# PSUM accumulators as pairs of banks for plain groups and as single banks for the seven products

## The chip, the core and the metric

The kernel runs as one program on one NeuronCore of a Trainium2 chip. The metric is device time in microseconds (us) from start to end of one execution. The core has TensorE (PE, matrix products), VectorE (DVE), ScalarE (ACT), GpSimd (POOL) and SyncE (SP), each of which works through its own instructions in order; waits between them are semaphores. TensorE writes its results into PSUM, which this kernel uses as 8 banks of 128 x 512 f32; DVE and ACT read them from there.

## The reference

One layer of a decoder step over 512 prompt positions and 8 sample positions that share weights (520 columns in all, `T`). The input is normalised and multiplied by one wide weight matrix `w_in`; its columns feed an attention branch (A), a gated mixing branch (B) and two merge gates:

```
h = rmsnorm(x, norm_in_g) @ w_in            # split into q, k, v, q_idx, w_idx, k_idx, z_a, u, v_b, z_b, g_a, g_b
o_a = sparse attention over the top-k keys  ;  o_b = u * (tril(W_s) @ layernorm(v_b) + b)
y_a = (o_a * silu(z_a)) @ w_proj_a          ;  y_b = (o_b * silu(z_b)) @ w_proj_b
mix = sigmoid(g_a) * y_a + sigmoid(g_b) * y_b
y   = rmsnorm(x + mix @ w_out, norm_f_g)
```

All of it is f32. What matters here is the part with `z_a`, `g_a` and `g_b`: 520 x 2048 times 2048 x 256 products, one for each 256 columns of `w_in`.

## The kernel before

**Precision.** Each f32 product is three passes: both operands are split into a high and a low part (`whi`, `wlo` for weights, `hT_hi`, `hT_lo` for the normalised input, which lies transposed in SBUF), and high x high, low x high and high x low are added in PSUM.

**Chunks.** The work of TensorE is a list of chunks, made once by `build()`. A plain group is 256 weight columns: two halves of 128, each in one or two chunks of 8 contraction tiles. Its result, 128 x 520, needs two banks (260 columns in each), so `pair_banks()` gives it a PSUM tile `pm` of 128 x 2 x 512; the pool `psm` holds two such tiles, four banks. The other four banks are the pool `pss` of small single-bank tiles (transposes, attention, sample work), which the change leaves alone.

**Seven products.** 17 groups in the middle of the list (two of `z_a`, seven of `g_b`, eight of `g_a`) use a scheme with seven products of half-size operands instead of eight. A group is seven chunks in the order `SEVEN`; a chunk is 8 contraction tiles x 3 passes = 24 matmuls that write 128 x 260, one bank. So there are 119 such chunks in a row, 2856 matmuls, all at line 338. For them `one_bank()` hands out the two banks of one `pm` tile in turn: the first chunk of a pair takes a new tile and its bank 0, the second takes bank 1 of the same tile. The right-hand operands are `hT_hi`/`hT_lo` quadrants or prepared sums `Fh`/`Fl`. Before the 119 chunks stands a plain group of `g_b`, behind them come the plain groups of `w_proj_a` (operands `oh`/`ol`), then `w_out`.

**What follows a chunk.** `seven_after` (lines 367 to 385) takes the finished bank out of PSUM: depending on the step ACT copies it to `s` or `c` (lines 367, 369, 372), or DVE adds it to an `s` or `c` tile (all DVE work has line 86, that of a helper). Step 5 adds two more DVE operations over `c` and `s` and an activation (line 381), step 6 another (line 385).

**Order.** The loop at the end of the kernel writes the order by hand. Before chunk i's matmuls it issues the split of the weights of chunk i+3 and the evacuation of chunk i-1:

```
while seven and ahead < i + SLOOK:                          # SLOOK = 3
    ahead += 1
    split(ahead, then=follow if pending else None)          # follow() issues the evacuation of chunk i-1
follow()
ps = main_chunk(i, ...)
```

Within a split of a seven chunk the order is: ACT rounds the raw weights to `whi` (line 257), then the evacuation of chunk i-1 (`then`), then DVE computes `wlo`, then up to two DVE additions `raw<-raw` that make the operand of a later step. Splits of plain chunks (the last three before the list leaves the seven chunks) have ACT `whi` and DVE `wlo` both ahead of the evacuation. `whi` and `wlo` have four buffers each, so the split of chunk i+3 starts when TensorE is through with chunk i-1.

**Waits.** Semaphore waits are not in the source. They follow from which instruction touches which tile: a matmul that writes into a PSUM tile waits for earlier readers of that tile, and the first write into a tile of a pool waits for the release of what lay there before.

Of the kernel before, what the change touches and what calls it, by code (L numbers as in the profile page):

```python
# [6 lines left out]
F32 = mybir.dt.float32  # L7
# [7 lines left out]
P = 128  # L15
# [45 lines left out]
def kernel(  # L61
# [31 lines left out]
    wspl = ctx.enter_context(tc.tile_pool(name="wspl", bufs=4))  # L93
    pools = {}
    dram = ctx.enter_context(tc.tile_pool(name="scratch", bufs=1, space=bass.MemoryType.DRAM))
    psm = ctx.enter_context(tc.tile_pool(name="psm", bufs=2, space=bass.MemoryType.PSUM))
    pss = ctx.enter_context(tc.tile_pool(name="pss", bufs=4, space=bass.MemoryType.PSUM))
    ctx.enter_context(tc.manual_schedule())
    half = {}


    def pair_banks():
        return psm.tile([P, 2, 512], F32, name="pm")

    def one_bank():
        if "t" in half:
            return half.pop("t")[:, 1, :]
        half["t"] = pair_banks()
        return half["t"][:, 0, :]

    xp = x_prompt[0]
    xs = x_sample.rearrange("b o d -> (b o) d")
# [191 lines left out]
    def rows_chunk(ch):  # L304
        hi, lo = spl_tiles["rows", ch["kq"]]
        c = ch["c"]
        if c is None and ch["first"]:
            state["ps"] = [pair_banks() for _ in range(2)]
        elif ch["first"]:
            state["ps"] = SB("rowp")  # L310
        for k in range(4):
            if k == 2:
                for job in state.pop("mid", ()):
                    next(job)
                    start(job)
            rh, rl = ch["rhs"](ch["kq"] * 4 + k)
            for u in range(2) if c is None else (0,):
                for j, (w, a) in enumerate(((hi, rh), (hi, rl), (lo, rh))):
                    flags = dict(start=ch["first"] and k == 0 and j == 0, stop=ch["last"] and k == 3 and j == 2)
                    if c is None:  # L320
                        nc.tensor.matmul(state["ps"][u][:, 0, :COLS_N], lhsT=w[:, k, u * P:(u + 1) * P],  # L321
                                         rhs=a[:, :COLS_N], **flags)
                    else:
                        nc.tensor.matmul(state["ps"][:, :2 * P], lhsT=a[:, off(c):off(c) + P], rhs=w[:, k, :], **flags)  # L324
        return state["ps"]

    def main_chunk(i, hook=None):
        ch = chunks[i]
        if ch["rows"]:
            return rows_chunk(ch)  # L330
        if ch.get("seven"):
            ps = one_bank()
            out = ps[:, :HALF]
            hi, lo = spl_tiles.pop((ch["raw"], ch["step"]))
            for k in range(8):
                rh, rl = ch["group"]["forms"](ch["f"], k)
                for j, (w, a) in enumerate(((hi, rh), (hi, rl), (lo, rh))):
                    nc.tensor.matmul(out, lhsT=w[:, k, :], rhs=a, start=k == 0 and j == 0,  # L338
                                     stop=k == 7 and j == 2)
            return ps  # L340
        if ch["first"]:
            state["ps"] = pair_banks()
        ps = state["ps"]
        hi, lo = spl_tiles.pop((ch["raw"], ch["u"]))
        for k in range(8):
            kt = ch["kc"] * 8 + k
            if hook is not None:
                hook(kt)
            rh, rl = ch["rhs"](kt)
            passes = ((hi, rh), (hi, rl), (lo, rh))[:2 if ch["evac"] is packed else 3]  # L350
            for j, (w, a) in enumerate(passes):
                for t0, t1, bank, o in ch["cuts"]:
                    nc.tensor.matmul(ps[:, bank, o:o + t1 - t0], lhsT=w[:, k, :], rhs=a[:, t0:t1],  # L353
                                     start=(ch["first"] and k == 0 and j == 0),
                                     stop=(ch["last"] and k == 7 and j == len(passes) - 1))
        return ps
# [1396 lines left out]
    while jobs:  # L1753
        for j in list(jobs):
            if next(j, 0) == 0:
                jobs.remove(j)


_INS = ["x_prompt", "x_sample", "cache_k", "cache_v", "cache_k_idx", "page_table", "norm_in_g", "w_in",
# [24 lines left out]
```

## Time and profile before

| | us |
|---|---|
| median of three runs | 1613.24 (1610.81 to 1613.37) |
| the profiled execution | 1622.19 |
| its span in the profile | 1620.5 |
| PE busy | 1512.1 (93%) |
| DVE busy | 982.9 (61%) |
| ACT busy | 580.3 (36%) |
| POOL busy | 314.3 (19%) |
| mean granted TensorE clock | 0.987 of full speed |

Times in the rows count from the span's start. A matmul's row shows its whole passage (0.28 us at full clock), and consecutive ones overlap: TensorE's pace is read from one start to the next. The clock is granted at full speed (2.4 GHz) or half (1.2 GHz).

### The profile page before, as it was taken

How to read it: one execution, taken by the hardware profiler on the slowest of the kernel's cores; microseconds unless marked ns; L12 is line 12 of the kernel's file. 1: busy time of each engine (PE TensorE's matmuls, PEld its weight loads, DVE VectorE, ACT ScalarE, POOL GpSimd, SP SyncE). 2: the span in 40 equal slices, each digit the busy share in tenths (PEclk: the TensorE clock that was granted, in tenths of full speed). 3: DMA queues.
4: the chain of work that ended last, by engine and by line, in shares of the span. 5: the costliest groups of instructions: out<-in, count | busy, mean ns of one | idle time of the engine just before them, and what ended most of it. 6: DMA issues, size and time to landing. Idle time of an engine off the chain costs nothing. (4 is left out here: it accounts for less than half of the span.)

```text
span 1620.5 us, 28341 instructions
## 1 busy us (share of the span) xinstructions
PE 1512.1 (93%) x11814; PEld 1488.8 (92%) x11814; DVE 982.9 (61%) x1844; ACT 580.3 (36%) x929; POOL 314.3 (19%) x429
## 2 busy tenths in 40 slices
PE   5999999999999899999999888888888889999997
PEld 5999999999999899999999788887888889999997
DVE  7545458989997334557567667766666665523224
ACT  6534333333222133434433333333333342323323
POOL 3000027872000400055301001010000023201111
PEclk9999999999999999999999999999999999999999
DMA  6333334455232223247542334343232458532222
GB/s 190 127 111 105 104 114 137 131 170 134 79 130 79 94 72 112 72 140 239 164 151 96 120 99 157 100 136 111 92 125 85 137 183 280 186 122 88 70 79 106
DMA packets 156579, 203.63 MB, mean 126 GB/s; under 512 B 7684, under 2 KB 138108, under 8 KB 156444
## 3 DMA queue, kind: packets, MB, share of 16 engines
q1 hardware_dynamic: 136292, 139.74, 26.8%
q0 software_dynamic: 20160, 62.09, 11.5%
q8 instruction: 92, 1.51, 0.4%
q14 instruction: 35, 0.29, 0.1%
HBM read 176.90 MB, written 24.91 MB: 125 GB/s over the span
## 5 line engine op out<-in xcount | busy, mean ns | idle before, releaser
L86 DVE TENSOR_TENSOR wlo<-raw,whi 128x1024 fp32r<-128x1024 f32 (+2 forms) x311 | 386.3, 1243 | 134.8 <-ACT whi L141 74.5
L353 PE MATMUL pm<-hT_hi,whi 128*128 128x260 f32 (+1 forms) x1648 | 378.5, 297 | 2.0 <-issue 2.0
L353 PE MATMUL pm<-hT_lo,whi 128*128 128x260 f32 (+1 forms) x1648 | 370.2, 293 | 4.0 <-DVE hT_lo L86 2.4
L353 PE MATMUL pm<-hT_hi,wlo 128*128 128x260 f32 (+1 forms) x1632 | 365.3, 293 | 0.8 <-issue 0.8
L353 PEld LDWEIGHTS pm<-hT_lo,whi 128*128 128x128 f32 x1648 | 264.2, 189 | 5.9 <-DVE hT_lo L86 3.2
L353 PEld LDWEIGHTS pm<-hT_hi,whi 128*128 128x128 f32 x1648 | 264.4, 189 | 2.6 <-issue 1.9
L353 PEld LDWEIGHTS pm<-hT_hi,wlo 128*128 128x128 f32 x1632 | 261.0, 189 | 0.9 <-issue 0.9
L141 ACT ACTIVATE whi<-raw 128x1024 fp32r<-128x1024 f32 (+2 forms) x192 | 193.4, 1009 | 94.4 <-PE pm L353 74.8
L257 ACT ACTIVATE whi<-raw 128x1024 fp32r<-128x1024 f32 x119 | 126.0, 1059 | 260.3 <-PE pm L338 128.8
L338 PE MATMUL pm<-hT_hi,whi 128*128 128x260 f32 x544 | 162.0, 298 | 34.6 <-DVE c L86 30.3
L338 PE MATMUL pm<-hT_lo,whi 128*128 128x260 f32 x544 | 158.5, 291 | 0.0
L338 PE MATMUL pm<-hT_hi,wlo 128*128 128x260 f32 x544 | 158.2, 291 | 0.0
L338 PE MATMUL pm<-Fh,whi 128*128 128x260 f32 x408 | 118.6, 291 | 37.0 <-ACT s L367 14.0
L338 PEld LDWEIGHTS pm<-hT_hi,whi 128*128 128x128 f32 x544 | 107.6, 198 | 41.2 <-DVE c L86 28.9
L338 PEld LDWEIGHTS pm<-Fh,whi 128*128 128x128 f32 x408 | 77.5, 190 | 42.4 <-ACT s L367 15.9
L338 PE MATMUL pm<-Fl,whi 128*128 128x260 f32 x408 | 115.9, 284 | 0.0
L338 PE MATMUL pm<-Fh,wlo 128*128 128x260 f32 x408 | 115.6, 283 | 0.0
L338 PEld LDWEIGHTS pm<-hT_lo,whi 128*128 128x128 f32 x544 | 107.6, 198 | 0.0
L338 PEld LDWEIGHTS pm<-hT_hi,wlo 128*128 128x128 f32 x544 | 107.4, 198 | 0.0
L353 PE MATMUL pm<-oh,whi 128*128 128x260 f32 x512 | 103.5, 284 | 0.0
L353 PE MATMUL pm<-ol,whi 128*128 128x260 f32 x512 | 103.1, 283 | 0.0
L353 PE MATMUL pm<-oh,wlo 128*128 128x260 f32 x512 | 102.8, 282 | 0.0
(504 smaller groups left out, 2771.5 us busy)
## 6 DMA issues: line engine op xcount, KB each, us to landing
raw<-in_w_in_dram SPq DMA_DIRECT2D x91, 1024.0 KB, 5.0
raw<-in_w_out_dram SPq DMA_DIRECT2D x16, 1024.0 KB, 5.3
raw<-in_w_proj_b_dram SPq DMA_DIRECT2D x8, 1024.0 KB, 7.2
raw<-in_w_proj_a_dram SPq DMA_DIRECT2D x8, 1024.0 KB, 6.7
yd<-y POOLq DMA_DIRECT2D x16, 260.0 KB
ld<-yd POOLq DMA_DIRECT2D x16, 260.0 KB
sigd<-c POOLq DMA_DIRECT2D x16, 260.0 KB
ld<-sigd POOLq DMA_DIRECT2D x16, 260.0 KB
```

The source lines that it names most:

```text
L86: return f(out, *a, **k)
L141: nc.scalar.activation(hi, src, AF.Copy)
L257: nc.scalar.activation(hi, src, AF.Copy)
L338: nc.tensor.matmul(out, lhsT=w[:, k, :], rhs=a, start=k == 0 and j == 0, stop=k == 7 and j == 2)
L353: nc.tensor.matmul(ps[:, bank, o:o + t1 - t0], lhsT=w[:, k, :], rhs=a[:, t0:t1], start=(ch["first"] and k == 0 and j == 0), stop=(ch["last ...
```

## The change

`psm` is no longer opened once with two pairs. A function `banks(kind)` opens a pool of its own for each mode and closes the one before it when the mode changes: two pairs for plain chunks (and for the `w_out` rows), four single-bank tiles for the seven products. The same four banks are used in both. Over the list the mode changes twice: from pairs to singles before the first of the 119 chunks, and back before the first `w_proj_a` chunk.

```diff
-    psm = ctx.enter_context(tc.tile_pool(name="psm", bufs=2, space=bass.MemoryType.PSUM))
     pss = ctx.enter_context(tc.tile_pool(name="pss", bufs=4, space=bass.MemoryType.PSUM))
     ctx.enter_context(tc.manual_schedule())
-    half = {}
+    mains = {}
+
+    def banks(kind):
+        if mains.get("kind") == kind:
+            return
+        if "cm" in mains:
+            mains["cm"].__exit__(None, None, None)
+        mains["n"] = mains.get("n", 0) + 1
+        cm = tc.tile_pool(name=f"psm{mains['n']}", bufs=2 if kind == "pair" else 4, space=bass.MemoryType.PSUM)
+        mains.update(kind=kind, cm=cm, pool=cm.__enter__())
 
     def pair_banks():
-        return psm.tile([P, 2, 512], F32, name="pm")
+        banks("pair")
+        return mains["pool"].tile([P, 2, 512], F32, name="pm")
 
     def one_bank():
-        if "t" in half:
-            return half.pop("t")[:, 1, :]
-        half["t"] = pair_banks()
-        return half["t"][:, 0, :]
+        banks("one")
+        return mains["pool"].tile([P, 512], F32, name="pone")
...
+    mains["cm"].__exit__(None, None, None)
```

No instruction is added, removed or moved: on each of the five engines the two programs have the same instructions in the same order (8797 listed rows on PE in both). What differs is which tile a matmul writes, and so what it waits for. The number behind a name is that of the buffer.

TensorE where the first seven chunk ends and the second begins, before: both chunks write tile 9992.

```order
L338 MATMUL pm_9992<-hT_lo_93,whi_9844 128x260
L338 MATMUL pm_9992<-hT_hi_92,wlo_9845 128x260
L338 MATMUL pm_9992<-Fh_9197,whi_9912 128x260 [waits Activation_49]
L338 MATMUL pm_9992<-Fl_9198,whi_9912 128x260
L338 MATMUL pm_9992<-Fh_9197,wlo_9913 128x260 [waits DVE_49]
L338 MATMUL pm_9992<-Fh_9197,whi_9912 128x260
```

The same six now:

```order
L345 MATMUL pone_9996<-hT_lo_90,whi_9844 128x260
L345 MATMUL pone_9996<-hT_hi_89,wlo_9845 128x260
L345 MATMUL pone_10038<-Fh_9197,whi_9912 128x260
L345 MATMUL pone_10038<-Fl_9198,whi_9912 128x260
L345 MATMUL pone_10038<-Fh_9197,wlo_9913 128x260 [waits DVE_49]
L345 MATMUL pone_10038<-Fh_9197,whi_9912 128x260
```

The second chunk has a tile of its own, and its first matmul no longer waits for ScalarE; in the built program that wait was for the ACT copy of tile 9992 to `s`, the evacuation of the first chunk. The wait on DVE, for `wlo` of its own weights, stays.

TensorE where the fifth seven chunk ends and the sixth begins, before: again one tile, and a wait for VectorE.

```order
L338 MATMUL pm_10131<-hT_lo_93,whi_10025 128x260
L338 MATMUL pm_10131<-hT_hi_92,wlo_10026 128x260
L338 MATMUL pm_10131<-hT_hi_92,whi_10062 128x260 [waits DVE_49]
L338 MATMUL pm_10131<-hT_lo_93,whi_10062 128x260
L338 MATMUL pm_10131<-hT_hi_92,wlo_10063 128x260
L338 MATMUL pm_10131<-hT_hi_92,whi_10062 128x260
```

The same six now:

```order
L345 MATMUL pone_10137<-hT_lo_90,whi_10029 128x260
L345 MATMUL pone_10137<-hT_hi_89,wlo_10030 128x260
L345 MATMUL pone_10167<-hT_hi_89,whi_10067 128x260 [waits Activation_49]
L345 MATMUL pone_10167<-hT_lo_90,whi_10067 128x260
L345 MATMUL pone_10167<-hT_hi_89,wlo_10068 128x260 [waits DVE_49]
L345 MATMUL pone_10167<-hT_hi_89,whi_10067 128x260
```

Before, the sixth chunk's first matmul waited for the DVE addition that takes the fifth chunk out of tile 10131. Now it waits for an ACT instruction, by its count the copy that empties the bank four chunks back, and the third matmul waits for the DVE instruction that makes its own `wlo`.

At the two changes of mode the built program has these waits. The first matmul of the first seven chunk waited for the evacuation of the plain chunk result two tiles back; now it waits for the one just finished (`sg<-pm`, line 1249 before), since the whole pool of pairs must be free. The first matmul of the first `w_proj_a` chunk waited for the DVE evacuation of the last seven chunk but one; now it waits for that of the last one.

## Rows read from the trace of the kernel before

**Rows 1.** The page: busy us (share) x instructions of each engine

```profile
PE 1512.1 (93%) x11814; PEld 1488.8 (92%) x11814; DVE 982.9 (61%) x1844; ACT 580.3 (36%) x929; POOL 314.3 (19%) x429
```

**Rows 2.** Waits of PE, longest first: us in total, times, longest

```profile
PE pm L338 <- DVE c L86: 30.3, 25, 2.7
PE pm L338 <- ACT s L367: 14.0, 9, 3.1
PE pm L338 <- ACT c L372: 12.2, 9, 1.4
PE pm L338 <- ACT s L369: 10.8, 8, 1.4
...
PE pm L338 <- DVE s L86: 4.4, 8, 0.7
```

**Rows 3.** Stretches: us; busy us of PE, PEld, DVE, ACT, POOL; PEclk; DMA; GB/s

```profile
38.00:200.00 162.00, 161.96 (x947) 159.30 (x948) 80.13 (x126) 68.60 (x132) 2.09 (x3) 1.00 0.35 114
...
887.50:1328.60 441.10, 369.47 (x2857) 357.49 (x2856) 294.50 (x339) 168.05 (x217) 33.57 (x62) 0.97 0.37 121
```

**Rows 4.** Timeline of PE across two chunk boundaries: start, us, instruction [idle before]

```profile
1317.10 0.28 PE L338 MATMUL pm<-Fh,wlo 128*128 128x260 f32 x1
1317.22 0.28 PE L338 MATMUL pm<-hT_hi,whi 128*128 128x260 f32 x1
...
1319.97 0.28 PE L338 MATMUL pm<-hT_hi,wlo 128*128 128x260 f32 x1
1322.94 0.39 PE L338 MATMUL pm<-hT_hi,whi 128*128 128x260 f32 x1 [2.68 <-DVE c L86]
1323.17 0.28 PE L338 MATMUL pm<-hT_lo,whi 128*128 128x260 f32 x1
```

**Rows 5.** Timeline of DVE and of PE around one of the 2.3 us waits

```profile
959.67 2.49 DVE L86 TENSOR_TENSOR raw<-raw 128x1024 f32<-128x1024 f32 x2
962.07 0.42 DVE L86 TENSOR_TENSOR c<-pm,s 128x260 f32<-128x260 f32 x1
...
962.54 0.39 PE L338 MATMUL pm<-hT_hi,whi 128*128 128x260 f32 x1 [2.32 <-DVE c L86]
```

**Rows 6.** Stretches: around a drop of the clock, then two of 50 us

```profile
895.10:898.40 3.30, 3.30 (x18) 3.30 (x17) 3.13 (x4) 0.45 (x1) 0.00 (x0) 0.50 0.67 235
...
1100.00:1150.00 50.00, 41.95 (x338) 40.54 (x337) 34.98 (x41) 18.81 (x24) 3.19 (x6) 1.00 0.34 112
1150.00:1200.00 50.00, 41.96 (x325) 40.54 (x324) 31.51 (x35) 17.94 (x23) 1.64 (x4) 0.97 0.33 106
```

**Rows 7.** Timeline at the first seven chunk, PE and ACT

```profile
887.53 0.28 PE L338 MATMUL pm<-hT_hi,whi 128*128 128x260 f32 x1
...
888.77 0.58 ACT L1249 ACTIVATE sg<-pm 128x520 f32<-128x520 f32 x1
...
893.25 0.37 ACT L367 ACTIVATE s<-pm 128x260 f32<-128x260 f32 x1
...
893.67 0.39 PE L338 MATMUL pm<-Fh,whi 128*128 128x260 f32 x1 [3.09 <-ACT s L367]
```

**Rows 8.** Timeline at the last seven chunk, DVE and PE

```profile
1327.13 1.22 DVE L86 TENSOR_TENSOR wlo<-raw,whi 128x1024 fp32r<-128x1024 f32 x1 [3.64 <-ACT whi L141]
...
1329.87 0.43 DVE L86 TENSOR_TENSOR c<-pm,c 128x260 f32<-128x260 f32 x1
...
1328.64 0.28 PE L338 MATMUL pm<-hT_hi,wlo 128*128 128x260 f32 x1
1328.84 0.47 PE L353 MATMUL pm<-oh,whi 128*128 128x260 f32 x2
```

**Rows 9.** DVE in 887.5 to 1328.6 by groups: count, busy us, mean ns, idle before

```profile
L86 DVE TENSOR_TENSOR wlo<-raw,whi 128x1024 fp32r<-128x1024 f32 x120 | 146.7, 1223 | 59.5 <-ACT whi L257 52.5 <-ACT whi L141 7.0
L86 DVE TENSOR_TENSOR raw<-raw 128x1024 f32<-128x1024 f32 x66 | 80.9, 1225 | 2.3
```

**Rows 10.** The page's weight loads: KB each, us from issue to landing

```profile
raw<-in_w_in_dram SPq DMA_DIRECT2D x91, 1024.0 KB, 5.0
```

## The prediction

> **What bounds the kernel now.** I read the page's table of engines first: PE is busy 93% of the span, DVE 61% [rows 1], so only PE's waits are worth time, and 108 us of the span are not PE work. The list of PE's waits says where most of those 108 us lie: five kinds of wait at line 338, the seven products, 30.3 + 14.0 + 12.2 + 10.8 + 4.4 = 71.7 us in 25 + 9 + 9 + 8 + 8 = 59 waits [rows 2]. Each is for an evacuation out of PSUM (DVE into `c` or `s`, ACT into `s` or `c`), none for weights or for a transfer. The view by stretches then shows what the stage is worth: in the 441.1 us of the seven products PE runs 2857 matmuls at a mean clock of 0.97, DVE is busy 294.5 us and ACT 168.0 [rows 3]. Last, the timeline. At 1317.22 a chunk begins 0.12 us behind the matmul before it, the ordinary step; the next chunk begins at 1322.94, 2.97 us behind the one at 1319.97, and PE sat idle for 2.68 us of that [rows 4]. 59 waits over 119 chunks is every second boundary: the second chunk of each pair, which writes the other bank of the tile that is just being emptied. First chunks of a pair, which take a fresh tile, do not wait.
>
> Why the wait is long is seen on DVE: an evacuation that DVE could do in 0.42 us starts at 962.07, behind two additions of raw weights that occupied DVE for 2.49 us from 959.67, and PE goes on at 962.54 after 2.32 us of idling [rows 5]. TensorE thus pays for the place of the evacuation in another engine's order.
>
> **The change part by part.** It removes and adds no instruction; it changes waits in three places.
>
> First, inside the seven products. Chunk i has a bank of its own and waits for the evacuation of chunk i-4, which is issued ahead of chunk i-3 and has three chunks' time to finish. The 59 waits go. I size this from the stage's own pace. A chunk without a wait takes 1319.97 - 1317.22 + 0.12 = 2.87 us [rows 4]; 119 of them are 341.5 us. The stage lasts from 887.53 [rows 7] to 1328.84 [rows 8], 441.3 us. The difference is 99.8 us. The parts confirm it: 71.7 us of waits as listed; for each wait 0.16 us more, since the list counts from the end of a 0.28 us passage and the next step would have come after 0.12, 9.4 us; the second matmul behind a wait comes 0.23 us after the first instead of 0.12 [rows 4], 6.5 us; and the clock, granted at half speed in stretches such as 895.10 to 898.40, where 3.30 us hold 18 matmul rows [rows 6]: a mean of 0.97 over 441.1 us is 0.03 x 441.1 = 13 us lost. Together 100.6 us.
>
> Do the drops of the clock go too? In 1100 to 1150 us no drop falls and 338 matmuls run; in 1150 to 1200 one does, and 325 run [rows 6]. The first drop stands right behind the longest wait, 3.09 us to 893.67 [rows 7]. In 38 to 200 us, where PE is busy 161.96 of 162.00 us, the clock stays at 1.00 [rows 3]. I take it that without waits it stays there: all 13 us return. Bounds: none of it to all of it.
>
> Second, the first seven chunk. The pool of pairs must be empty before the singles open, so its first matmul, now at 887.53, waits for the sigmoid of the last plain chunk, which on ACT starts at 888.77 and takes 0.58 us. A matmul released by ACT starts 0.05 us behind its end (893.25 + 0.37 to 893.67) [rows 7]: 889.40, so 1.87 us, and 0.11 for the start after a wait. Queued behind the waiting matmul is all of PE's stage, so the price is paid in full. Bounds: 0, if the sigmoid came earlier, which its place behind a `whi` excludes; and 3.6 us, if the wait costs a drop of the clock (half of a 3.3 us stretch as in [rows 6] lost). It cannot be a gain, since PE has nothing else to do.
>
> Third, the first `w_proj_a` chunk waits for the evacuation of the last seven chunk. DVE does it at 1329.87, 0.43 us long [rows 8], the last of five operations in its queue since 1327.13; with the same 0.05 us PE would go on at 1330.35 instead of 1328.84: 1.5 us, plus 0.11. The last chunk but one no longer waits its 2.68 us [rows 4], but DVE's five operations hang on that chunk's end in either program, so the distance stays. Bounds: 0 to 3.2, as above.
>
> What is late next? On DVE, 294.5 / 17 = 17.3 us of work per group of seven chunks against 7 x 2.87 = 20.1 us [rows 3]: 86%, no longer slack by a third. Its longest burst is the split of a first step: `wlo` and two additions, 1.22 + 2.49 us [rows 5, 9], behind an evacuation of 0.42, and begun some 1.1 us after the chunk's end because `whi` comes first; that is 5.2 us against a chunk of 2.87, so DVE falls 2.4 us behind and recovers in the two light steps that follow. The `wlo` is wanted three chunks later, 8.6 us, and the bank too. ACT has 168.0 / 17 = 9.9 us per group. The weights: two loads of 1024 KB per group at 5.0 us each [rows 10] are 10 us of 20.1, and the tighter one, issued after the fourth step's split, is needed at the next group's first split, four chunks or 11.5 us later. I take nothing for any of these.
>
> Sum: -99.8 + 1.98 + 1.6 = -96.2 us on the profiled execution, 1622.19 (span 1620.5), that is 1526.0. That execution stands 9.0 us over the median of the runs, 1613.24; I carry the same difference and predict 1517 us.
>
> **The rivals.**
>
> A, DVE becomes the bound of the stage. For it: 86% of the new stage, and `wlo` already has 59.5 us of idling for `whi` in front of it [rows 9]. If all of that idling survived, the stage could not be shorter than 294.5 + 59.5 = 354 us, 12.5 more than 341.5: 1530 us. Against it: that idling is mostly DVE being early.
>
> B, the clock goes on dropping. The step from one accumulator to another is a short pause at each chunk, and if such pauses, not the waits of 1.4 to 3.1 us, cost the clock, the 13 us stay: 1530 us. The boundary at 1317.22, one of 60 that take a fresh tile today, has no pause at all [rows 4], which speaks against it. The Trainium skill, "TensorE: Matmul & The Clock Gate", section "A second HAM failure mode: psum-queue depth-cycling", tells of a kernel that cycled through PSUM banks at each iteration and whose clock swung between its two levels because of micro-idles between groups; by that rule four banks in rotation would keep the drops, and the sum would be 1530. This trace agrees that idling between groups goes with drops, but not that taking another bank makes it.
>
> C, nothing changes. If four accumulators are too few, in whatever shape, PE waits for the oldest one and the same 72 us appear under another name: 1613 us. For it: the number of banks is the same. Against it: the wait is always for the chunk just finished, never for an older one, and the built program asks for the one four back.
>
> D, slower. With its waits gone PE draws on for 342 us without a pause while DVE and ACT are busier than elsewhere, and the clock could be granted at half speed for long. At that level a matmul takes 3.30 / 16 = 0.21 us or so (18 rows touch the stretch, two of them at its edges) against 0.12, a chunk 5.0 us. The loss passes the gain when 96 / (5.0 - 2.87) = 45 of 119 chunks run so; if all did, 1517 + 119 x 2.1 = 1767 us. Against it: 162 us of unbroken work at 1.00, with DVE busy half the time [rows 3].
>
> **How the numbers follow.** Forecast 0.77; A 0.09; B 0.06; C 0.04; D 0.02; 0.02 for what I have not thought of. The forecast's own range is 1512 (both mode changes free, the clock's loss at the upper end of its rounding) to 1524 (both cost a drop of the clock, some chunks wait briefly). A and B give 1530; 1512 to 1536 holds both and leaves out C, D and heavier forms of A. No change means within 0.2%, some 3 us, about what a measurement of this kernel can tell: C and half of the rest, 0.05. Faster is the forecast, A, B and the other half, 0.93; slower is D, 0.02.
>
> **What would show it.** In the new trace PE's waits at the seven products' line should be gone but for one of about 1.9 us at the first chunk, and one of about 1.5 us should stand before the first `w_proj_a` matmul; the stage should last about 345 us at a clock of 0.99 or 1.00; 50 us of it should hold some 420 matmuls; all other stages should keep their lengths. A wait for `wlo` or `whi` at chunk starts would show A, a clock of 0.97 without waits B, waits on evacuations C. The forecast is wrong if the stage stays above 360 us.

## The result, and the profile after

The changed kernel took 1521.41 us (four runs: 1517.78, 1517.96, 1524.87, 1525.2), the kernel before, beside it, 1613.3 (1610.81 to 1619.57): a ratio of 0.9425, 95% interval 0.9384 to 0.9466. Forecast were 1517 us in a range of 1512 to 1536. The profiled execution took 1525.2 us, forecast for a profiled one were 1526.0; before it was 1622.19.

The page's row of engines, which answers to [rows 1]:

```profile
PE 1485.7 (98%) x11814; PEld 1473.5 (97%) x11814; DVE 978.9 (64%) x1844; ACT 580.5 (38%) x929; POOL 315.4 (21%) x429
```

PE has as many instructions as before and is busy for 26 us less, since a matmul's passage is longer behind a wait and at half clock. From the list of PE's waits (us in total, times, longest), the rows that touch the stage; the 59 waits of [rows 2] are not in it any more. The seven products' matmul is now at line 345 and writes `pone`, the plain one is at line 360:

```profile
PE pm L360 <- DVE hT_lo L86: 2.4, 1, 2.4
PE pone L345 <- ACT sg L1256: 1.7, 1, 1.7
PE pm L360 <- DVE c L86: 1.5, 1, 1.5
```

The wait for `hT_lo` was there before, far from this stage. The other two are the changes of mode. The timeline at the first chunk of the stage, at the boundary to the second, and at the last (start, us, instruction, idle before), for [rows 4, 7, 8]:

```profile
885.66 0.40 PE L360 MATMUL pm<-hT_hi,wlo 128*128 128x260 f32 x2
887.13 0.58 ACT L1256 ACTIVATE sg<-pm 128x520 f32<-128x520 f32 x1
887.77 0.39 PE L345 MATMUL pone<-hT_hi,whi 128*128 128x260 f32 x1 [1.71 <-ACT sg L1256]
...
890.63 0.28 PE L345 MATMUL pone<-hT_hi,wlo 128*128 128x260 f32 x1
890.75 0.28 PE L345 MATMUL pone<-Fh,whi 128*128 128x260 f32 x1
...
1228.07 1.22 DVE L86 TENSOR_TENSOR wlo<-raw,whi 128x1024 fp32r<-128x1024 f32 x1 [0.70 <-ACT whi L148]
...
1229.60 0.28 PE L345 MATMUL pone<-hT_hi,wlo 128*128 128x260 f32 x1
1230.82 0.43 DVE L86 TENSOR_TENSOR c<-pone,c 128x260 f32<-128x260 f32 x1
1231.39 0.48 PE L360 MATMUL pm<-oh,whi 128*128 128x260 f32 x2 [1.51 <-DVE c L86]
```

The boundary at 890.75 is the one at which PE idled 3.09 us in [rows 7]. Now the first matmul of the second chunk follows 0.12 us behind the last of the first. PE leaves the sigmoid's wait 0.06 us behind the sigmoid's end (887.13 + 0.58), and the last wait 0.14 us behind the evacuation's.

The view by stretches, for [rows 3, 6] (us; busy us of PE, PEld, DVE, ACT, POOL; granted clock; DMA share; GB/s):

```profile
887.60:1229.60 342.00, 341.83 (x2855) 341.83 (x2856) 289.11 (x338) 166.68 (x215) 33.58 (x62) 1.00 0.48 154
...
1000.00:1050.00 50.00, 50.00 (x420) 50.00 (x420) 43.01 (x52) 23.80 (x30) 4.28 (x8) 1.00 0.49 154
```

From its first matmul to the first of `w_proj_a` the stage takes 1231.39 - 887.77 = 343.6 us, before 1328.84 - 887.53 = 441.3. With the wait in front of it (885.66 + 0.24 to 887.77, 1.87 us) that is a saving of 95.8 us of the 97.0 between the two profiled executions. But for that wait the stage begins 1.6 us earlier (a stretch near 550 us, told below, lost 1.9 us less), and what stands behind it takes 0.5 us longer. The weights arrive at 154 GB/s instead of 121 and PE never waits for one.

DVE's groups in the stage, for [rows 9] (count, busy us, mean ns, idle before and what ended it):

```profile
L86 DVE TENSOR_TENSOR wlo<-raw,whi 128x1024 fp32r<-128x1024 f32 x120 | 146.6, 1222 | 35.9 <-ACT whi L264 33.5 <-ACT whi L148 2.5
```

The same work, with 35.9 us of idling for `whi` in front of it instead of 59.5.

One thing must be known to read single times. In some executions, of the kernel before and of the kernel after alike, PE stutters near 550 us. The same 30 us of an execution of the kernel before, of one of the kernel after, of one of the kernel after in a later run (1518.3 us, below), and of the last two runs told below (the kernel before, and the kernel before with its additions spread):

```profile
540.00:570.00 30.00, 25.59 (x188) 24.78 (x187) 5.66 (x6) 5.10 (x6) 12.89 (x14) 0.89 0.28 89
```

```profile
540.00:570.00 30.00, 27.13 (x204) 25.90 (x203) 6.34 (x7) 5.22 (x6) 13.06 (x15) 0.94 0.31 98
```

```profile
540.00:570.00 30.00, 30.00 (x252) 30.00 (x251) 7.53 (x7) 6.28 (x7) 13.68 (x15) 1.00 0.34 104
```

```profile
540.00:570.00 30.00, 25.12 (x173) 23.79 (x173) 4.43 (x4) 4.16 (x5) 12.25 (x14) 0.89 0.28 89
```

```profile
540.00:570.00 30.00, 25.86 (x164) 24.19 (x163) 4.37 (x4) 3.67 (x4) 12.69 (x14) 0.77 0.28 89
```

252 matmuls in 30 us are 0.119 us each; 188 and 204 of them are 64 and 48 too few, 7.6 and 5.7 us lost, and by the same count the last two executions lost 9.4 and 10.5. That place is in plain groups, which the change does not touch, and it is what parts the 1518 and the 1525 us above, so far as the profiles show (only one execution of each set of runs has one).

### The profile page after: what moved, and what is told of

Read it like the earlier page. It is cut to its first block, busy times and chain, and to the rows that moved or that the text cites. A ratio compares the mean times of both kernels' runs of the same rounds, so it can differ in the third digit from the quotient of the medians.

```text
span 1523.5 us, 28390 instructions
## 1 busy us (share of the span) xinstructions
PE 1485.7 (98%) x11814; PEld 1473.5 (97%) x11814; DVE 978.9 (64%) x1844; ACT 580.5 (38%) x929; POOL 315.4 (21%) x429
## 5 line engine op out<-in xcount | busy, mean ns | idle before, releaser
L360 PEld LDWEIGHTS pm<-hT_lo,whi 128*128 128x128 f32 x1648 | 264.2, 189 | 5.9 <-DVE hT_lo L86 3.2
L360 PEld LDWEIGHTS pm<-hT_hi,whi 128*128 128x128 f32 x1648 | 264.0, 189 | 0.8 <-issue 0.2
L360 PEld LDWEIGHTS pm<-hT_hi,wlo 128*128 128x128 f32 x1632 | 260.8, 189 | 1.5 <-issue 1.5
L345 PE MATMUL pone<-hT_hi,whi 128*128 128x260 f32 x544 | 153.7, 283 | 1.7 <-ACT sg L1256 1.7
L345 PE MATMUL pone<-hT_hi,wlo 128*128 128x260 f32 x544 | 153.5, 282 | 0.0
L345 PE MATMUL pone<-hT_lo,whi 128*128 128x260 f32 x544 | 153.4, 282 | 0.0
L345 PE MATMUL pone<-Fh,wlo 128*128 128x260 f32 x408 | 115.2, 282 | 0.0
L345 PE MATMUL pone<-Fl,whi 128*128 128x260 f32 x408 | 115.1, 282 | 0.0
L345 PE MATMUL pone<-Fh,whi 128*128 128x260 f32 x408 | 115.1, 282 | 0.0
L345 PEld LDWEIGHTS pone<-hT_hi,whi 128*128 128x128 f32 x544 | 102.4, 188 | 1.9 <-ACT sg L1256 1.9
```

## The experiments

My theory: two consecutive chunks that lie in one tile are tied, the second waits for the first one's evacuation, and any layout that parts them removes the whole of it. The rivals: it is the number of accumulators that counts; it is the place of the evacuation in the queues of DVE and ACT; and the clock's share is something else than a consequence of the waits. The first four kernels ran beside one another (before: 1611.37 us).

**Two single banks instead of four.** In the kernel after:

```diff
-        cm = tc.tile_pool(name=..., bufs=2 if kind == "pair" else 4, ...)
+        cm = tc.tile_pool(name=..., bufs=2 if kind == "pair" else 2, ...)
```

> The changed kernel with two single banks instead of four for the seven products. Theory (the loss was that two neighbouring chunks share one tile, so that a chunk waits for the evacuation of the one just finished): a chunk now waits for the evacuation two chunks back, which DVE and ACT finish within 2.3 us of that chunk's end, inside the 2.87 us of the chunk between; so no waits in the stage, its length 345 to 348 us as with four, time 1518 to 1526. Rival (what helped is the depth of four accumulators): with two the waits come back at least in part, some 72 us of PE waits for evacuations in the stage, a stage of 400 us or more, time 1580 or more.

It took 1518.33 us (1518.13 to 1518.43), ratio 0.9420 (0.9405 to 0.9436). The stage, by the view of stretches:

```profile
880.60:1224.60 344.00, 342.46 (x2857) 342.08 (x2857) 290.62 (x340) 167.24 (x216) 33.55 (x62) 1.00 0.49 155
```

Busy for all but 1.5 us at full clock, as with four. An evacuation needs to be done within one chunk's time, and it is. The depth of four earns nothing here.

**One single bank.**

```diff
-        cm = tc.tile_pool(name=..., bufs=2 if kind == "pair" else 4, ...)
+        cm = tc.tile_pool(name=..., bufs=2 if kind == "pair" else 1, ...)
```

> The changed kernel with a single bank for the seven products: every chunk waits for the evacuation of the one just finished, 118 waits instead of 59. Theory: the price of each step is that of before (idle 1.5 us behind an ACT evacuation, 0.7 behind a DVE one, 0.8 for the first step, and for the sixth the 2.5 us of before less what the wait ahead of it already gave DVE, 1.7), 8.4 us and 7 x 0.1 for starting again in each of 17 groups: 155 us over the 341.5 without waits, a stage of about 497 us, time about 1670 to 1685. If drops of the clock come with any wait, they double, and it is 20 us more. Rival (the waits of before were not for the tile): the stage stays near 345 us.

It took 1682.86 us, ratio 1.0441 (1.0421 to 1.0462): every boundary waits. PE's waits:

```profile
PE pone L345 <- DVE c L86: 48.5, 50, 2.7
PE pone L345 <- ACT s L374: 23.1, 17, 1.4
PE pone L345 <- ACT c L379: 23.0, 17, 1.4
PE pone L345 <- ACT s L376: 22.9, 17, 1.4
PE pone L345 <- DVE s L86: 11.0, 17, 2.7
```

118 waits, 128.5 us listed. The stretches: the whole stage, most of it without its ends, and three spells near its end:

```profile
880.80:1388.50 507.70, 378.63 (x2856) 354.44 (x2856) 295.02 (x340) 167.01 (x216) 33.56 (x62) 0.99 0.33 105
...
1000.00:1350.00 350.00, 262.39 (x2010) 245.40 (x2009) 204.81 (x231) 114.37 (x147) 19.36 (x37) 1.00 0.32 100
...
1368.20:1371.50 3.30, 3.30 (x17) 3.30 (x17) 0.29 (x1) 0.00 (x0) 0.00 (x0) 0.50 0.00 0
1375.30:1378.30 3.00, 3.00 (x14) 3.00 (x15) 0.54 (x1) 0.00 (x0) 0.00 (x0) 0.50 0.75 212
1382.50:1387.70 5.20, 5.20 (x24) 5.20 (x24) 1.00 (x2) 0.64 (x1) 0.00 (x0) 0.50 0.00 0
```

The stage is 164.1 us longer than with four. Some 6 of them are not waits: the three spells at half clock hold 11.5 us of work, half of it lost. The rest is about 158 / 118 = 1.34 us per wait where the list has 128.5 / 118 = 1.09; the prediction's 0.16 + 0.11 us per wait on top of the list make 1.36. So the list understates a wait by about a quarter of a microsecond, and the prediction's way of adding that is confirmed on another kernel. The time lies in the range expected, but the stage does not: some 497 us were expected and 507.7 measured. The clock came out against the case in which drops come with any wait: PE waits at twice as many boundaries as before, and yet the clock is 1.00 through the middle of the stage, where before it was 0.97 over the whole of it. The longest wait of those 350 us, on PE's timeline (the others are of 1.5 us at most):

```profile
1341.28 0.39 PE L345 MATMUL pone<-hT_hi,whi 128*128 128x260 f32 x1 [2.13 <-DVE c L86]
```

The matmul behind it takes the 0.39 us of full clock. Only behind the last waits, of 2.7 us, does the clock fall to half, as in the last three stretches shown.

**The evacuation ahead of the split, in the kernel before.** If place in the queue is the cause, putting the evacuation first should do as well:

```diff
         if then is not None:
-            next(steps, 0)
             then()
```

> The kernel before, pairs shared by two chunks as they were, but each evacuation is issued ahead of the weight split and not behind its ScalarE part. Theory: the 59 waits stay, but each lasts only as long as the evacuation: 0.6 to 0.8 us, apart from the nine behind the two additions of raw weights on DVE, which stay near 2 us. 50 x 0.68 + 9 x 2 + 59 x 0.11 = 58 us over 341.5, and up to 13 us if the clock goes on dropping: a stage of 400 to 413 us, time 1573 to 1588. If the drops of the clock come from the longest waits alone, eight or nine may stay, or fewer where those fall under 2 us. Rival (the length of a wait is not set by what stands ahead of the evacuation): stage 441, time 1613.

1602.8 us (1602.61 to 1603.16), ratio 0.9945 (0.9929 to 0.9962): I missed. Against the 1613 us named there the gain was to be 25 to 40 us; it is 8.6. PE's waits, to be held against [rows 2]:

```profile
PE pm L337 <- DVE c L86: 37.6, 25, 2.3
PE pm L337 <- ACT c L371: 10.1, 9, 1.7
PE pm L337 <- ACT s L366: 6.0, 9, 2.2
...
PE pm L337 <- ACT s L368: 3.8, 8, 0.5
```

The waits for ACT fell from 37.0 to 19.9 us. Those for DVE's `c` rose from 30.3 to 37.6. DVE and PE around one of them:

```profile
1051.60 2.48 DVE L86 TENSOR_TENSOR raw<-raw 128x1024 f32<-128x1024 f32 x2
1054.00 0.42 DVE L86 TENSOR_TENSOR c<-pm,s 128x260 f32<-128x260 f32 x1
...
1054.48 0.39 PE L337 MATMUL pm<-hT_hi,whi 128*128 128x260 f32 x1 [2.33 <-DVE c L86]
```

The two additions of the split before still stand ahead of the evacuation, as in [rows 5]: what I moved is the head of the next split, `whi` on ACT, so only ACT's order changed, and DVE got its `whi` later: it idles 88.4 us for `whi` in front of the stage's `wlo`, where before it idled 59.5 [rows 9]:

```profile
L86 DVE TENSOR_TENSOR wlo<-raw,whi 128x1024 fp32r<-128x1024 f32 x119 | 145.5, 1223 | 88.4 <-ACT whi L257 87.0 <-ACT whi L141 1.2
```

The mistake was to read the source and not DVE's order. Place in the queue does set the length of a wait, but this edit did not change the place that matters.

**The pool of singles reopened at the first of every seven chunks.** In the kernel after:

```diff
-    def one_bank():
+    def one_bank(step):
+        if step == 0:
+            mains["kind"] = None
         banks("one")
...
-            ps = one_bank()
+            ps = one_bank(ch["step"])
```

> The changed kernel, but the pool of four singles is closed and opened again ahead of each of the 17 groups of seven products. Theory (a newly opened pool waits until everything in the one before it is evacuated): the first chunk of 16 groups waits for the evacuation of the chunk just finished, 0.7 to 0.8 us and 0.1 to start again: 13 us in all, a stage of 358 to 360 us, profiled time 1535 to 1539 where the changed kernel's profiled execution took 1525. Rival (only the bank that is taken must be free, which was emptied three chunks ago): no change, 1518 to 1526.

1535.83 us, ratio 0.9529 (0.9510 to 0.9548), and a stage of 359.1 us, both in the ranges expected. Stage, waits, and one of them:

```profile
882.90:1242.00 359.10, 345.27 (x2857) 342.29 (x2857) 290.84 (x340) 167.29 (x216) 33.57 (x62) 1.00 0.47 149
```

```profile
PE pone L347 <- DVE c L86: 12.3, 16, 1.3
```

```profile
1030.16 0.36 PE L347 MATMUL pone<-hT_hi,whi 128*128 128x260 f32 x1 [0.73 <-DVE c L86]
```

16 reopenings, 16 waits for the evacuation of the chunk just finished, 359.1 - 343.6 = 15.5 us, 1 us each (13 us in all were expected). A pool that is opened over another's banks waits until the last of these is read, three of four banks being free or not. That is the price of a change of mode, which the kernel after pays twice.

**The changed kernel again, and pairs handed out in turn.** These two ran together (before: 1612.79 us). The second keeps the kernel before with its one pool of pairs, and only takes the four halves in another order: A0, B0, A1, B1 instead of A0, A1, B0, B1:

```diff
     def one_bank():
-        if "t" in half:
-            return half.pop("t")[:, 1, :]
-        half["t"] = pair_banks()
-        return half["t"][:, 0, :]
+        n = half["n"] = half.get("n", -1) + 1
+        if n % 4 < 2:
+            half[n % 2] = pair_banks()
+        return half[n % 2][:, n % 4 // 2, :]
```

> The changed kernel once more, beside the next one. Both theories: as before, 1518 to 1525, with a wait of 1.7 us at the first seven chunk and one of 1.5 us at the first w_proj_a chunk. Executions with a disturbed stretch near 550 us take some 7 us more than those without, in every kernel seen.

> The kernel before, one pool of two pairs throughout, but the four banks handed out in another order: bank 0 of one tile, bank 0 of the other, bank 1 of the first, bank 1 of the second, and then the two tiles again. No pool is reopened. Theory (neighbouring chunks must not share a tile; a chunk that waits for the one two back does not wait): no waits in the stage, and none at its two ends, since no pool has to be empty: 342 us from its first matmul to the first of w_proj_a, 3.4 us less than the changed kernel's 345.6 from the last plain matmul, time 1513 to 1516. Rival (it is the shape, single-bank tiles in a pool of their own, that helps; tiles of two banks that two chunks share make them wait): waits at the shared tiles as before, 1600 or more.

The changed kernel took 1519.61 us (1518.30 to 1520.88), ratio 0.9423 (0.9410 to 0.9436), which overlaps with that of two singles; pairs in turn 1516.25 us (1515.73 to 1517.41), ratio 0.9403 (0.9390 to 0.9416), below every run of the changed kernel and just over the 1513 to 1516 us expected. The stage of pairs in turn, and, on PE's timeline, its ends and the two waits in it:

```profile
878.50:1222.10 343.60, 342.78 (x2858) 342.10 (x2857) 290.69 (x340) 167.99 (x217) 33.67 (x62) 1.00 0.49 154
```

```profile
878.20 0.40 PE L353 MATMUL pm<-hT_hi,wlo 128*128 128x260 f32 x2
878.43 0.28 PE L338 MATMUL pm<-hT_hi,whi 128*128 128x260 f32 x1
...
884.58 0.39 PE L338 MATMUL pm<-Fh,whi 128*128 128x260 f32 x1 [0.23 <-ACT s L367]
...
891.12 0.39 PE L338 MATMUL pm<-hT_hi,whi 128*128 128x260 f32 x1 [0.54 <-ACT c L372]
...
1221.88 0.28 PE L338 MATMUL pm<-hT_hi,wlo 128*128 128x260 f32 x1
1222.02 0.47 PE L353 MATMUL pm<-oh,whi 128*128 128x260 f32 x2
```

Both changes of mode are free: no pool is closed, PE goes from one tile to the next in the ordinary step of 0.12 us (the row at 878.20 holds two matmuls) and in 0.14 us. In exchange a half waits for the half of its tile two chunks back, which makes PE idle twice, both times in the first group, for 0.23 and 0.54 us. That, with the restarts, is most of why the stage takes 343.6 us and not the 342 expected. From the last plain matmul before the stage to the first of `w_proj_a` it takes 343.7 us against 345.6 after the change, so 1.9 us of the 3.4 us between the medians are placed. The two profiled executions differ by 2.5 us, and there another 0.5 us lie ahead of the stage; the rest is between other executions and stays open. This version is as good as the change (0.2% faster than the changed kernel beside it), and it shows that neither single banks nor the reopened pool is what earns the 93 us: chunks that follow one another must lie in different tiles, and that is all.

**The kernel before again, and its additions spread.** The last two ran together (before: 1621.72 us; the profiles of this set have the stutter near 550 us). They ask what the clock's share hangs on. The first is the kernel before, unedited, for a second profile. The second moves one of the two additions that stand ahead of the evacuation to the next step, so that the 2.3 us waits become about 1.1 us; the waits ahead of a seventh chunk may grow a little:

```diff
             if step == 0:
                 add(b11, b11, b12)
+            elif step == 1:
                 add(b12, b12, b22)
```

> The kernel before, once more, for a profile without the disturbed stretch near 550 us that its first one had. Theory (the stage of the seven products costs what the first profile showed): from the last plain matmul ahead of it to the first w_proj_a matmul 441 us, with eight or nine drops of the clock in it, span 1613 to 1615. If the medians' difference of 93 us is the truth and the profile's 97 an accident of that one execution, the stage is 2 to 3 us shorter here: 438 to 439, with a drop or two less.

> The kernel before, with one edit: of the two DVE additions on raw weights that follow a first step's split, the second is issued behind the next step's split. The pairs stay shared, the 59 waits stay. Nine of them (ahead of a sixth chunk) shrink from 2.3 us to about 1.1, since one addition of 1.22 us less stands in front of the evacuation: 11 us. Eight others (ahead of a seventh chunk) may grow by 0.6 us: 5 us. Theory (the clock drops only behind the long waits): no drop is left in the stage after its first 10 us, 10 to 12 us more: time 1612 - 11 + 5 - 11 = 1595, 1591 to 1599. Rival (drops come with the waits as such, long or short): they stay, 1603 to 1608.

The kernel before: 1619.72 us, ratio 0.9984 (0.9956 to 1.0013). Its stage:

```profile
888.40:1326.70 438.30, 366.66 (x2858) 354.65 (x2857) 294.55 (x340) 167.95 (x217) 33.55 (x62) 0.98 0.38 122
```

The waits are those of [rows 2], yet it is 3.0 us shorter than in the first profile, as the second of the two cases expected has it. (A profile without the stutter was hoped for; this one has it, so the span forecast with it can't be compared.) Three of the eight waits of 2.3 us on PE's timeline, each in the same place of its group of seven:

```profile
1013.44 0.39 PE L338 MATMUL pm<-hT_hi,whi 128*128 128x260 f32 x1 [2.33 <-DVE c L86]
...
1063.51 0.39 PE L338 MATMUL pm<-hT_hi,whi 128*128 128x260 f32 x1 [2.31 <-DVE c L86]
...
1115.16 0.55 PE L338 MATMUL pm<-hT_hi,whi 128*128 128x260 f32 x1 [2.32 <-DVE c L86]
```

From the first to the second it is 50.07 us, from the second to the third 51.65, with the same work and the same waits: a spell at half clock costs 1.5 to 1.6 us (two spells less made the stage 3.0 us shorter), and it follows one such wait and not another. Counted by these distances, in the first profile eight of the ten waits of 2.3 us and more were followed by a drop, here six; the longest wait, 3.1 us at the first pair, was followed by one there and not here. So the size of the gain hangs in part on the execution that one happened to profile.

The additions spread: 1607.87 us (1597.57 to 1610.02), ratio 0.9921 (0.9893 to 0.9949), 13.9 us less; I had expected 17, the rival 4 to 9. As a plain time it falls in the rival's range of 1603 to 1608 us, since both stand on a kernel before at 1612 us and the one beside it took 1621.72; so the stage decides, not the time. Its stage behind the first chunks, and the same place in a group as [rows 5]:

```profile
901.00:1313.80 412.80, 350.76 (x2803) 338.94 (x2801) 284.45 (x328) 160.41 (x207) 32.32 (x60) 1.00 0.40 126
```

```profile
959.33 1.22 DVE L86 TENSOR_TENSOR raw<-raw 128x1024 f32<-128x1024 f32 x1
...
960.94 0.39 PE L339 MATMUL pm<-hT_hi,whi 128*128 128x260 f32 x1 [1.06 <-DVE c L86]
```

PE's waits that changed:

```profile
PE pm L339 <- DVE c L86: 20.2, 25, 2.7
...
PE pm L339 <- DVE s L86: 8.0, 8, 1.3
```

The waits as listed fell by 30.3 - 20.2 for `c` and rose by 8.0 - 4.4 for `s`: 6.5 us net. From the last plain matmul to the first of `w_proj_a` the stage now takes 424.3 us, before 438.4 and 441.4 in its two profiles: 14.1 to 17.1 us less. The rest, 7.6 to 10.6 us, is the clock: it is 1.00 from 901 us on, with nearly all of the 59 waits still there, only shorter, and 7.6 to 10.6 us are five to seven drops at 1.5 (one of the six or eight is left, behind the first wait, ahead of 901 us). So shortening the 2.3 us waits takes the drops with it, though PE goes on waiting at every second boundary.

## Why the prediction was right, and where its size was off

**The waits.** Shown. All 59 go, as forecast, and they go with the layout alone: with two singles, with four, and, but for two short ones in the first group, with pairs in turn. The built order had said that the chunk asks for the bank four back; the runs show that two back is far enough.

**The stage's pace.** 119 chunks at 2.87 us were to take 341.5 us. From 887.77 to the step after 1229.60 it is 1229.72 - 887.77 = 341.95 us, and 50 us hold 420 matmuls, the number forecast.

**The clock.** Shown by three kernels. I took all of 13 us to return, since the drops stood behind waits; the stage after is at 1.00, and spreading the additions brought 7.6 to 10.6 us back without removing a single boundary's wait. The size was that of one execution: eight drops at 1.5 to 1.6 us are 12 to 12.6 us, six are 9 to 9.5. My 13 us came from a clock of 0.97 that was rounded, so the term is up to 1 us high for that execution and 3.5 to 4 us for the second. The sum does not rest on the 13 us, since its 99.8 us are a difference of two measured times, but the drops are in that difference too.

**The changes of mode.** 1.87 + 0.11 and 1.5 + 0.11 us were forecast; beyond the ordinary step, 1.87 us and 1231.39 - 1229.72 = 1.67 us were measured. Neither brought a drop of the clock.

**DVE, ACT and the loads at nothing.** Shown: DVE is busy 289.11 of 342.00 us, 85%, and PE waits for no `whi`, no `wlo` and no weight.

**The sum.** -96.2 us forecast for the stage and its ends, -95.8 measured; 1526.0 us forecast for a profiled execution, 1525.2 measured. So close an agreement is partly luck of the execution: the size was read from a profile with eight drops and held against the same profile. With the 438.3 us of the second profile the same working gives 3.0 us less, 93.2, and the medians that ran beside each other differ by 93.0 (two singles) and 93.2 us (the changed kernel again); that fits, but one execution of each set is too few to show it.

**The carry to the median** is the term that was mis-sized. I took the profiled execution to stand 9.0 us over the median, as before. Of those 9.0 us the stutter near 550 us makes up 7.6, and it comes in some executions only: in two of the four of the kernel after, if the 7 us between them are that, so the median fell between, 3.5 us over the executions without it, 1518 us. I had seen the difference of 9.0 us and had not asked where in the trace it lies; a stretch of plain groups at a clock of 0.89, with seven waits of 4.4 us in all put down to "issue", was there to be found. What causes it stays open: no kernel here was made for it.

**The rivals.** A (DVE the bound, 1530 us) falls: of the 59.5 us of idling for `whi` 35.9 remain, and none reaches PE. B (the clock goes on dropping, 1530 us) falls: the kernel after takes another bank every 2.87 us at a granted clock of 1.00, and so do two singles and the pairs in turn. The rule named there, in the Trainium skill, "TensorE: Matmul & The Clock Gate", section "A second HAM failure mode: psum-queue depth-cycling", speaks of frequent micro-idles between groups as the cause. The runs agree only in part: the drops went when the idling did, but with one single bank PE idled 0.5 to 1.5 us, once 2.13, at every boundary for 350 us at a clock of 1.00. Changing banks alone brought no drop, and frequent short idles brought none either. C (four accumulators too few, 1613 us) falls by the kernel after and by two singles. D (half clock for long, up to 1767 us) falls: DVE at 85% and PE at 100% of the stage went together with a clock of 1.00.

## What to carry to other kernels

A tile of two banks is one thing to whoever waits for it: give consecutive accumulation groups different tiles, and if the pool's shape is fixed, take its halves in turn (A0, B0, A1, B1); two accumulators were enough here, and opening another pool over the same banks cost a full drain of 1 to 2 us each time. When an evacuation must wait behind other work, a move has to be judged by the order of the engine that evacuates. And before a profiled time is carried to a median, find the stretch in which the two differ.

## What the runs showed of the hardware that was not expected

In the stage the clock fell to half only behind single long idles, eight times in one execution and six in another behind the same ten waits of 2.3 to 3.1 us, and not in the 350 us with a wait at every chunk boundary, the longest of them 2.13 us and the others 1.5 at most. The same wait is followed by a drop in one execution and not in another. And plain groups can stutter for some 10 us with nothing to wait for that the profile shows, at a loss of 6 to 10 us in four of the ten profiles (188, 204, 173 and 164 matmuls in 30 us where 252 fit).
